# Attention with a second, filling stream of matmuls: maxima earlier, stores later, more filler

## Chip, cores, metric

One core of one Trainium2 chip runs the kernel. The metric is the device time of one execution in microseconds (us); lower is better. Engines: PE multiplies matrices, DVE, ACT and POOL work on elements, and SP does nothing here but issue DMAs from one queue, in order.

## The reference, cut to what matters

```python
u = rms_norm(x, norm_g)                      # [2048, 1024]
q, k, v, z_att, f, z_ssd, xbc, dt, x_lru, z_lru = split(u @ w_in)
# A) 8 heads of 64, causal, with a forget bias c = cumsum(log_sigmoid(f + forget_b))
logits = q_i @ k.T * 64**-0.5 + (c_i[:, None] - c[None, :])   # masked above the diagonal
y_att = softmax(logits) @ v * silu(z_att)                     # 512 columns
y_ssd = ...                                                    # 1024 columns, gated norm at the end
y_lru = ...                                                    #  512 columns
out = x + concat([y_att, y_ssd, y_lru]) @ w_out                # w_out [2048, 1024]
```

## The kernel before

Everything is float32; a product is made of three float32r matmuls, of high and low halves (h·h, h·l, l·h). Up to about 1250 us of the span the kernel makes the projections, the LRU and SSD branches and the normalised q and k, and leaves them in DRAM. This part is not touched. Then follow two streams of work that share the PE.

**Attention.** A *unit* `j` is a head `h` and a block `sb` of 256 queries; there are 64, the blocks of head 0 and head 7 in falling order and those of the six heads between in rising order. A unit has `sb + 1` *tasks* `(j, kp)`, one for each 256 keys: 288 in all. `score(j, kp)` makes the transposed scores of a task in a PSUM bank `T` (L987, L988), ACT takes their exponential twice (L996 rounded into `ph`, L997 in full), and DVE takes the difference `pl` (L998). Three tasks later (`AVL`) `av` multiplies with the values into `O` (L1040, L1042), and `finish` closes the unit: the sums of the exponentials go in through `ah` and `al` (L1050, L1051), the result `to` (L1054 to L1058) and the sums `su` go to DRAM (L1061, L1063). The diagonal task of a unit, its last, uses 384 of the bank's 512 columns and gets a mask matmul (L992).

The exponential needs each query's extreme score beforehand. `maxima(j)` makes plain scores `S` on PE (L945) in chunks of 512 keys, and DVE reduces each (L955, or L950 for the chunk at the diagonal, L953 over the chunks) into a column of `mz`. `flip(j)` transposes `mz` on PE (L969) into a PSUM tile `pm`, and two ACT casts (L970, L971) put it as a row into `q`, which the first score matmul of unit `j` reads (L987). `S` and `pm` share two PSUM banks (`psS`), `T` has three, `O` two, the filler one.

**Filler.** `sweeps()` is a generator that makes the output projection: per 128 tokens `t` and half `n` of the columns, four *rounds* of three matmuls of 512 columns (L1112 to L1114, `po`), and DVE adds the result to `xr`, which came from DRAM and goes back there (`pt_d`; L1133, L1118 or L1120, L1135). `mix` loads and splits the left operand (`mt`, `mh`, `ml`). Sweep 0 takes the LRU rows, sweep 1 half of the SSD rows; then the other half and the attention rows alternate. There are 512 rounds. `fill` draws rounds while attention runs, `FIRST + tasks * RATE // 288` of them, and the rest follow when attention is over. `load_wo` loads a fourth of `w_out` in eight pieces and splits each on ACT and DVE.

The order of the instructions on each engine is set by the framework's scheduler, from the order in which the code creates them; each engine then runs its list in order. What a list holds is shown below where it matters.

Of the kernel before, what the change touches and what calls it, by code (L numbers as in the profile page):

```python
# [18 lines left out]
P = 128  # L19
# [11 lines left out]
FIRST = 12  # L31
RATE = 260
LEAD = 3
# [5 lines left out]
AVL = 3  # L39
LT = 2  # L40
NDV = 3
# [7 lines left out]
def hybrid_block(ctx, tc, x, norm_g, w_in, q_norm_g, k_norm_g, forget_b, ssd_conv_w, ssd_conv_b,  # L49
# [338 lines left out]
    def group_za(pool, vpool, g):  # L388
        w = weights([(C_ZA + g * 256, 256)])
        for tb in range(4):  # L390
            for mm in range(2):
                m = g * 2 + mm
                ps = proj_ch(w, mm, tb, f"pza{m}_{tb}")
                if g == 1 and tb == 2 and mm == 0:
                    anchor[1] = anchor[0]
                th = pool.tile([P, 512], F32, name=f"th{m}_{tb}", tag="sqq")
                A.activation(th, ps, AF.Tanh, scale=0.5)
                zt = vpool.tile([P, 512], F32, name=f"zt{m}_{tb}", tag="qk")
                V.scalar_tensor_tensor(zt, th, 1.0, ps, op0=ALU.add, op1=ALU.mult)
                dma(za_d[m][:, tb * 512:(tb + 1) * 512], zt)  # L400

# [374 lines left out]

    for i in range(2):
        G.memset(mzs[i], 0.0)
    for i in range(2):
# [41 lines left out]

    def load_wo(k0, half, lastp, tag):
        ws = {}
        pl = [(k0 + i, n) for i in range(4) for n in range(2)]
        tags = [f"u{p}{half}_{k}" for k in range(KD) for p in "hl"]
        for j, (k, n) in enumerate(pl):
            h = upa.tile([P, 512], F32R, name=f"woh{k}_{n}", tag=tags[2 * j])
            l = upa.tile([P, 512], F32R, name=f"wol{k}_{n}", tag=tags[2 * j + 1])
            cs = slice(n * 512, n * 512 + 512)
            row = w_out[k * P:(k + 1) * P, cs]  # L830
            if j + 1 < len(pl):
                raw = [upa.tile([P, 512], F32, name=f"wor{k}_{n}", tag=tags[2 * j + 3])]
            else:
                raw = [lastp.tile([P, 256], F32, name=f"wor{k}_{n}_{i}", tag=tag) for i in range(2)]
            m = 512 // len(raw)
            for i, r in enumerate(raw):
                dma(r, row[:, i * m:(i + 1) * m])
                hc, lc = h[:, i * m:(i + 1) * m], l[:, i * m:(i + 1) * m]
                if 4 <= k < 12:
                    g = c1("sg", k - 4)  # L840
                    A.activation(hc, r, AF.Copy, scale=g)
                    V.scalar_tensor_tensor(lc, r, g, hc.bitcast(F32), op0=ALU.mult,
                                           op1=ALU.subtract)
# [4 lines left out]
        return ws  # L848

    with tpool(name="ap", bufs=2) as pool, tpool(name="ap1", bufs=1) as ap1, \  # L850
            tpool(name="qkp", bufs=QB) as qkp:
        for p in range(4):
# [41 lines left out]
            if p == 2:  # L894
                load_head(0)
                load_q(0)
    ws = [load_wo(12, 0, wrp, "wr"), load_wo(8, 1, wrp, "wr")]
    pb.close()

    pcx = ExitStack()  # L900
    o2 = cx.enter_context(tpool(name="o2", bufs=2))
    o3 = cx.enter_context(tpool(name="o3", bufs=LEAD))
    a1 = cx.enter_context(tpool(name="a1", bufs=1))
# [9 lines left out]
    make_k2(1)  # L913
    make_q(a1)
    U = [{} for _ in units]

    def maxima(j):
# [6 lines left out]
        def first():  # L924
            if j % 2 and j + 1 < len(units):
                load_q(j + 1)
            za = a3.tile([64, 256], F32, name=f"za{j}", tag="za")
            u["za"] = za
            p, b = divmod(h, 2)
            dma(za, za_d[p][b * 64:b * 64 + 64, sb * 256:(sb + 1) * 256])  # L930
            if j % 8 == 2 and h < 7:
                load_head(h + 1)

        def chunk(i, c0):
# [5 lines left out]
            o = (sb % 2) * 256 + i * P  # L940
            col = mzs[j % 2][:, 64 + 32 * i:65 + 32 * i]
            if c0 == 0 and nc_ > 1:
# [5 lines left out]
            if c0 + w == n:  # L948
                jk = a1.tile([P, 512], F32, name=f"jk{j}_{i}", tag="jk")
                V.tensor_tensor_reduce(jk[:, 0:w], ps[:, 0:w], zm[:, 640 - w:640], 1.0, 3.0e38,  # L950
                                       ALU.add, ALU.min, to)
                if nc_ > 1:
                    V.tensor_reduce(col, u["mc"][:, 0:nc_], axis=AX.X, op=ALU.min)  # L953
            else:
                V.tensor_reduce(to, ps, axis=AX.X, op=ALU.min)  # L955
# [6 lines left out]

    def flip(j):

        h, sb = units[j]
        q3 = qs_[j // 2][0]
        o = (sb % 2) * 256
        pm = psS.tile([P, P], F32, name=f"pm{j}", tag="S")
        T.transpose(pm[0:97, :], mzs[j % 2][:, 0:97], ident)  # L969
        A.copy(q3[96:97, o:o + P], pm[64:65, :])  # L970
        A.copy(q3[96:97, o + P:o + 256], pm[96:97, :])  # L971

    def score(j, kp):
# [71 lines left out]
    def finish(j):  # L1045
# [17 lines left out]
        dma(s_d[qt, h:h + 1, :].rearrange("i o t -> o i t"),  # L1063
            su.rearrange("o (i t) -> o i t", i=2))
        if h == 7:

            sr = a2.tile([16, P], F32, name=f"sr{j}", tag="sr")
# [10 lines left out]
    def mix(t, k0, kind):  # L1078
# [5 lines left out]
        if kind == "att":  # L1084
            dma(mt, at_d[:, :, tsl].rearrange("i p t -> p i t"))
            rb = o2.tile([P, 4, P], F32, name=f"rb{t}", tag="xr")
            for b in range(2):
# [34 lines left out]
    SEQ = ((12, "lru"), (8, 1), (4, 0), (0, "att"))  # L1122

    def sweeps():
        for i in range(2):
            cur = mix(0, *SEQ[i])
            for t in range(NT):
                nxt = mix(t + 1, *SEQ[i]) if t + 1 < NT else None
                tsl = slice(t * P, (t + 1) * P)
                for n in range(2):  # L1130
                    cs = slice(n * 512, n * 512 + 512)
                    xr = o2.tile([P, 512], F32, name=f"xr{t}_{n}_{i}", tag="xr")
                    dma(xr, (pt_d if i else xf)[tsl, cs])  # L1133
                    yield from half(t, n, i, cur, xr)
                    dma(pt_d[tsl, cs], xr)  # L1135
                cur = nxt
            ws.append(load_wo(SEQ[i + 2][0], i, o2, "mt"))

        xs = {}
        work = [(t, 2) for t in range(LEAD)]  # L1140
# [6 lines left out]
        for w, (t, i) in enumerate(work):  # L1147
            tsl = slice(t * P, (t + 1) * P)
            if i == 2:
                xs[t] = o3.tile([P, D], F32, name=f"xo{t}", tag="xo")  # L1150
                dma(xs[t], pt_d[tsl, :])
            if i == 3 and cur is None:
                cur = mix(t, *SEQ[3])
            nxt = None
            for n in range(2):
                cs = slice(n * 512, n * 512 + 512)
                if n == 1 and w + 1 < len(work) and (work[w + 1][1] == 2 or "X" in pso):
                    nxt = mix(work[w + 1][0], *SEQ[work[w + 1][1]])
                yield from half(t, n, i, cur, xs[t][:, cs])
                if i == 3:  # L1160
                    dma(of[tsl, cs], xs[t][:, cs])
            cur = nxt

    filler = sweeps()
    with tc.high_priority(offset=HP), tc.issue_after(anchor[1].ins):
        steps = maxima(0)
        for j, st in enumerate(steps):
            st()
            for _ in range(FIRST * (j + 1) // len(steps) - FIRST * j // len(steps)):
                next(filler)  # L1170
        flip(0)
    count = [0, FIRST]
    recent = []

    def fill(ins):
        count[0] += 1
        recent.append(ins)
        want = FIRST + count[0] * RATE // 288
        while want > count[1]:
            count[1] += 1  # L1180
            with tc.issue_after(recent[max(0, len(recent) - 1 - LAG)].ins):
                next(filler)

# [8 lines left out]
    flips = {begin[j] - 1: j for j in range(1, len(units))}  # L1192
    for i in range(len(tasks) + AVL + 1):
        ins = None
        if i < len(tasks):
            ins = score(*tasks[i])
            if i in flips:
                flip(flips[i])
            for f in at.get(i, ()):
# [7 lines left out]
        if ins is not None:  # L1207
            fill(ins)
    pcx.close()
    pso["P"] = cx.enter_context(tpool(name="psP2", bufs=6, space=PSUM))  # L1210
# [33 lines left out]
```

## Time and profile before

| | us |
|---|---|
| median of 3 runs (lowest, highest) | 2072.73 (2069.95, 2073.84) |
| profiled execution, its time | 2065.23 |
| profiled execution, span | 2063.5 |
| PE busy, share of the span | 1970.9, 96% |
| DVE, ACT, POOL busy | 1303.0, 1007.7, 803.1 |
| first maxima of the first unit (L945) start | 1231.3 |
| last mask matmul (L992) starts | 1889.7 |

A row of the groups reads: line, engine, operation, output<-inputs, shapes, count | busy us, mean ns of one | idle us of the engine just before them, and what ended it. A row of the waits reads: who waited <- for whom: us in total, times, longest. A row of the windows gives a stretch, its length, busy us and instructions of each engine, the clock that PE was granted (1.00 is full speed), and the share and rate of the DMA engines. A matmul's end in the profile is modelled, and one that streams starts long before the one ahead of it has ended.

### The profile page before, as it was taken

To read this page: it belongs to the slowest core of one execution; us is meant where nothing else is said; L and a number is where in the kernel's file an instruction comes from. 1 tells how busy PE (TensorE), PEld (TensorE's weight loads), DVE (VectorE), ACT (ScalarE), POOL (GpSimd) and SP (SyncE) were. 2 spreads that over 40 slices of the span, in tenths; PEclk is the share of its full clock that TensorE was granted. 3 is DMA by queue.
4 is the path that set the end of the run, shared out by engine and by line. 5 is a ranking of instruction groups with operands and counts; after the bars stand their busy time and mean duration, and the time that the engine had idled before them with its cause. 6 is when DMAs were issued, how large, how long until landed. Compare 5 with 4: busy or idle time off the path is not lost.

```text
span 2063.5 us, 35018 instructions
## 1 busy us (share of the span) xinstructions
PE 1970.9 (96%) x11941; PEld 1713.8 (83%) x11941; DVE 1303.0 (63%) x2576; ACT 1007.7 (49%) x2177; POOL 803.1 (39%) x918
## 2 busy tenths in 40 slices
PE   7999999999999999898999998989899999898999
PEld 6898888898989898787887986878777888777887
DVE  6748555555464736777667264777777777787343
ACT  7524444544443534544444242666576666675110
POOL 0100000233231415555553003768677777776110
PEclk9999999999999999999999998999999999999999
DMA  5322223121312145667756465355365455342554
GB/s 186 97 82 70 70 79 95 41 74 34 99 31 75 31 133 175 190 176 222 207 163 177 109 194 165 115 152 149 108 187 142 126 151 152 105 141 82 173 170 136
DMA packets 260466, 261.32 MB, mean 127 GB/s; under 512 B 26772, under 2 KB 198832, under 8 KB 258736
## 3 DMA queue, kind: packets, MB, share of 16 engines
q1 hardware_dynamic: 260128, 259.05, 42.7%
q8 instruction: 95, 1.56, 0.3%
q0 software_dynamic: 160, 0.03, 0.1%
q14 instruction: 83, 0.68, 0.1%
HBM read 164.22 MB, written 94.77 MB: 126 GB/s over the span
## 4 chain that ended last, share of the span: by engine, by line
PE 41%; DMA 6%; DVE 4%; ACT 4%; issue 2%; POOL 2%; SPq 0%; DVEq 0%; POOLq 0%; ACTq 0%
PE po L1112 5%; PE po L1113 5%; PE po L1114 5%; PE T L987 3%; PE T L988 3%; PE S L945 2%; PE O L1040 2%; PE O L1042 2%; PE py L691 2%; PE pza L358 1%; PE pza L359 1%; PE pza L357 1%; DMA ab<-acs_d 1%; PE pqk L341 1%; PE pqk L343 1%
## 5 line engine op out<-in xcount | busy, mean ns | idle before, releaser
L998 DVE TENSOR_TENSOR pl<-T,ph 128x512 fp32r<-128x512 f32 (+1 forms) x288 | 187.3, 655 | 48.8 <-ACT T L997 46.3
L1112 PE MATMUL po<-woh,mh 128*128 128x512 f32 x512 | 204.1, 399 | 7.5 <-DVE xr L1120 4.6
L996 ACT ACTIVATE ph<-T 128x512 fp32r<-128x512 f32 (+1 forms) x288 | 165.1, 573 | 88.7 <-PE T L988 60.5
L1113 PE MATMUL po<-wol,mh 128*128 128x512 f32 x512 | 202.7, 396 | 0.0
L1114 PE MATMUL po<-woh,ml 128*128 128x512 f32 x512 | 202.6, 396 | 0.0
L1010 POOL TENSOR_TENSOR ac<-ac,ph 128x512 f32<-128x512 f32 x120 | 156.1, 1301 | 23.1 <-ACT ph L996 17.2
L997 ACT ACTIVATE T<-T 128x512 f32<-128x512 f32 (+1 forms) x288 | 164.9, 572 | 0.0
L987 PE MATMUL T<-q,k 128*128 128x256 f32 x576 | 150.0, 287 | 9.6 <-ACT q L971 6.8
L955 DVE TENSOR_REDUCE mc<-S 128x1 f32<-128x512 f32 x192 | 130.2, 685 | 41.8 <-PE S L945 41.3
L357 PE MATMUL pxx<-uh,wh 128*128 128x512 f32 x384 | 152.8, 400 | 1.7 <-ACT uh L302 1.7
L358 PE MATMUL pxx<-ul,wh 128*128 128x512 f32 x384 | 153.1, 399 | 0.0
L345 PE MATMUL pqk<-wh,ul 128*128 128x256 f32 x512 | 151.0, 295 | 0.0
L359 PE MATMUL pxx<-uh,wl 128*128 128x512 f32 x384 | 150.9, 395 | 0.0
L1040 PE MATMUL O<-ph,vv 128*128 128x256 f32 x576 | 149.0, 280 | 0.9 <-ACT ph L996 0.4
L343 PE MATMUL pqk<-wl,uh 128*128 128x256 f32 x512 | 148.8, 291 | 0.0
L341 PE MATMUL pqk<-wh,uh 128*128 128x256 f32 x512 | 148.6, 291 | 0.0
L1042 PE MATMUL O<-pl,vv 128*65 128x256 f32 x576 | 142.2, 279 | 3.4 <-DVE pl L998 2.8
L413 DVE SCALAR_TENSOR_TENSOR accx<-rtx,cv,accx 128x512 f32<-128x512 f32 x144 | 108.0, 752 | 57.3 <-ACT accx L410 54.5
L343 PE MATMUL pzs<-wl,uh 128*128 128x256 f32 x512 | 143.8, 281 | 0.0
L988 PE MATMUL T<-qx,kx 128*128 128x256 f32 x576 | 143.7, 283 | 0.0
L345 PE MATMUL pzs<-wh,ul 128*128 128x256 f32 x512 | 143.4, 280 | 0.0
L341 PE MATMUL pzs<-wh,uh 128*128 128x256 f32 x512 | 143.0, 281 | 0.0
(353 smaller groups left out, 5711.8 us busy)
## 6 DMA issues: line engine op xcount, KB each, us to landing
ab<-acs_d SPq DMA_DIRECT2D x64, 256.0 KB
pt_d<-xr SPq DMA_DIRECT2D x64, 256.0 KB
wr<-in_w_in_dram SPq DMA_DIRECT2D x112, 128.0 KB
xt<-in_x_dram SPq DMA_DIRECT2D x16, 512.0 KB
xs_d<-stx SPq DMA_DIRECT2D x32, 256.0 KB
v_d<-vs SPq DMA_DIRECT2D x32, 256.0 KB
wr<-in_w_in_dram SPq DMA_DIRECT2D x128, 64.0 KB
zs_d<-zs SPq DMA_DIRECT2D x32, 256.0 KB
```

The costliest lines, as they stand in the source:

```text
L341: T.matmul(ps[:, i, :], h[k][:, sl], wh[k], start=(k == 0 and i == 0), stop=False, skip_group_check=True)
L343: T.matmul(ps[:, i, :], h[k][:, sl], wl[k], start=False, stop=False, skip_group_check=True)
L345: ins = T.matmul(ps[:, i, :], l[k][:, sl], wh[k], start=False, stop=last, skip_group_check=True)
L358: T.matmul(ps, wh[k][:, ms], ul[tb][k], start=False, stop=False)
L987: T.matmul(ps, k2[:, ks], q3[:, qs], start=(jj == 0), stop=False, skip_group_check=True)
L988: ins = T.matmul(ps, kx[:, ks], qx[:, qs], start=False, stop=True, skip_group_check=True)
L998: V.tensor_tensor(pl[:, 0:n], pt[:, 0:n], ph[:, 0:n].bitcast(F32), op=ALU.subtract)
L1040: T.matmul(po[:, qs], vv[:, kt, 0:128], ph[:, cs], start=(kt == 0), stop=(kt == 2 * sb + 1), skip_group_check=True)
L1042: T.matmul(po[0:65, q2], vv[:, kt, 64:129], pl[:, cs], start=False, stop=False, skip_group_check=True)
L1112: T.matmul(ps, mh[:, j, :], h, start=(j == 0), stop=False)
L1113: T.matmul(ps, mh[:, j, :], l, start=False, stop=False)
L1114: T.matmul(ps, ml[:, j, :], h, start=False, stop=(j == 3))
```

## The change

- `LT` 2 to 3: a unit's maxima are made one task earlier. Four `mz` tiles of 97 columns instead of two of 128; `za` gets a fourth buffer.
- `flip(j + 1)` writes its transpose into columns 384 to 512 of the bank of the diagonal scores of unit `j`, right behind the mask matmul, instead of into a bank of `psS`.
- `load_head` of the next head moves from unit 2 of a head to unit 4.
- `finish` and the filler hand their stores to `later`, which issues them 1 or 2 tasks on; the reciprocals' round trip through DRAM follows the sums' store, and `ready` tells the filler 4 tasks later that the attention rows of this block can be mixed, which it now may do ahead.
- `xr` is loaded one half ahead, into four buffers instead of two.
- `load_wo` becomes a generator that loads a piece ahead and splits one piece at a time: the second fourth of `w_out` during sweep 0, no longer before attention; the third during sweep 1, the last behind it.
- `RATE` 260 to 290, and `MORE = 2` further rounds for each of the last `END = 14` tasks.
- The discarded output `jk` of L950 is bfloat16, and the store of `za` in `group_za` is created one step later.

```diff
-RATE = 260
+RATE = 290
-LT = 2
+LT = 3
+END = 14
+MORE = 2
...
-    mzs = [kc.tile([P, P], F32, name=f"mz{i}") for i in range(2)]
+    mzs = [a1.tile([P, 97], F32, name=f"mz{i}") for i in range(4)]
...
-            if j % 8 == 2 and h < 7:
+            if j % 8 == 4 and h < 7:
                 load_head(h + 1)
...
-    def flip(j):
+    def flip(j, pm):
...
-        pm = psS.tile([P, P], F32, name=f"pm{j}", tag="S")
-        T.transpose(pm[0:97, :], mzs[j % 2][:, 0:97], ident)
+        T.transpose(pm[0:97, :], mzs[j % 4], ident)
         A.copy(q3[96:97, o:o + P], pm[64:65, :])
         A.copy(q3[96:97, o + P:o + 256], pm[96:97, :])
...
             ins = T.matmul(pv, idr, zmt.unsqueeze(1).broadcast_to([P, 2, P]), start=False,
                            stop=True, skip_group_check=True)
+            if j + 1 < len(units):
+                flip(j + 1, pt[:, 384:512])
...
-        dma(at_d[p][b * 64:b * 64 + 64, cs], to)
...
+        def store():
+            dma(at_d[p][b * 64:b * 64 + 64, cs], to)
+            dma(s_d[qt, h:h + 1, :].rearrange("i o t -> o i t"),
+                su.rearrange("o (i t) -> o i t", i=2))
...
+            later(lambda: ready.add(sb), 4)
+
+        later(store, 1)
...
+    def later(f, n=2):
+        if clock[0] is None:
+            f()
+        else:
+            late.append((clock[0] + n, f))
...
-                    xr = o2.tile([P, 512], F32, name=f"xr{t}_{n}_{i}", tag="xr")
-                    dma(xr, (pt_d if i else xf)[tsl, cs])
+                    load_xr(t * 2 + n + 1)
+                    xr = xrs.pop(t * 2 + n)
                     yield from half(t, n, i, cur, xr)
-                    dma(pt_d[tsl, cs], xr)
+                    def store(xr=xr, t=t, n=n):
+                        dma(pt_d[t * P:(t + 1) * P, n * 512:n * 512 + 512], xr)
...
+                        later(store)
...
+                    if t > 0 and n == 0:
+                        next(more, None)
...
-                if n == 1 and w + 1 < len(work) and (work[w + 1][1] == 2 or "X" in pso):
-                    nxt = mix(work[w + 1][0], *SEQ[work[w + 1][1]])
+                if n == 1 and w + 1 < len(work):
+                    t1, i1 = work[w + 1]
+                    if i1 == 2 or t1 // 2 in ready:
+                        nxt = mix(t1, *SEQ[i1])
...
-        want = FIRST + count[0] * RATE // 288
+        want = FIRST + count[0] * RATE // 288 + MORE * max(0, count[0] - 288 + END)
```

Three places in the engines' lists show what this moves.

PE, around the transpose for unit 36 (a middle unit of head 4), before. `O35` is the output of unit 35, `T36_0` the first scores of unit 36, `S37` the maxima of unit 37:

```order
L945 MATMUL S37_0_0_18382<-k20_9585,q30_9577 128x512
L1042 MATMUL O35_18418<-pl35_3_18399,vv4_16897 65x256
L1040 MATMUL O35_18418<-ph35_3_18398,vv4_16897 128x128
L1042 MATMUL O35_18418<-pl35_3_18399,vv4_16897 65x128
L969 MATMUL pm36_18411<-ident_102,mz0_9573 97x128
L945 MATMUL S37_0_512_18415<-k20_9585,q30_9577 128x512
L987 MATMUL T36_0_18437<-q30_9577,k20_9585 128x256
L988 MATMUL T36_0_18437<-qx0_9580,kx4_16896 128x256
```

and after, from the mask matmul of unit 35 on:

```order
L1011 MATMUL T35_3_18417<-zmt_9571,idr_9569 128x2x128
L988 MATMUL T35_3_18417<-ident_102,mz0_13447 97x128
L1063 MATMUL O35_18448<-pl35_0_18328,vv4_17078 65x256
L1061 MATMUL O35_18448<-ph35_0_18327,vv4_17078 128x256
L1063 MATMUL O35_18448<-pl35_0_18328,vv4_17078 65x256
L1061 MATMUL O35_18448<-ph35_1_18361,vv4_17078 128x256
L1139 MATMUL po5_0_8_18521<-woh8_0_13806,mh5_8_18235 128x512
L1140 MATMUL po5_0_8_18521<-wol8_0_13807,mh5_8_18235 128x512
L1071 MATMUL O34_18337<-ah34_18304,onr_9566 65x256
L1141 MATMUL po5_0_8_18521<-woh8_0_13806,ml5_8_18236 128x512
L1139 MATMUL po5_0_8_18521<-woh9_0_14288,mh5_8_18235 128x512
```

Before, one matmul stands between the transpose and the scores that need it; after, `T36_0` is the eighteenth row behind the transpose.

ACT at the same place, before (`q30` is the casts' target):

```order
L996 ACTIVATE ph35_3_18398<-T35_3_18392 128x384
L997 ACTIVATE T35_3_18392<-T35_3_18392 128x384
L970 CAST q30_9577<-pm36_18411 1x128
L971 CAST q30_9577<-pm36_18411 1x128
L1021 CAST ah35_18407<-w35_18403 128x256
```

and after:

```order
L989 CAST q30_9573<-T35_3_18417 1x128
L990 CAST q30_9573<-T35_3_18417 1x128
L1017 ACTIVATE ph35_3_18426<-T35_3_18417 128x384
L1018 ACTIVATE T35_3_18417<-T35_3_18417 128x384
L1017 ACTIVATE ph36_0_18472<-T36_0_18467 128x512
```

The casts have moved ahead of the exponentials of the diagonal task, whose bank they read.

SP in sweep 0, before (`to15`, `su17` are results and sums of units 15 and 17):

```order
L930 DMA za19_15868<-za_d1_78 64x256
L1061 DMA at_d_97<-to16_15979 64x256
L1135 DMA pt_d_13500<-xr10_0_0_16003 128x512
L1133 DMA xr10_1_0_16134<-in_x_dram 128x512
L1096 DMA mt13_12_16557<-lr_d3_101 128x128
L1063 DMA s_d_93<-su17_16069 2x1x128
L1133 DMA xr11_0_0_16298<-in_x_dram 128x512
```

and after:

```order
L1190 DMA pt_d_13455<-xr9_0_0_15423 128x512
L1086 DMA s_d_93<-su13_15520 2x1x128
L1179 DMA xr11_0_0_15885<-in_x_dram 128x512
L1085 DMA at_d_97<-to13_15519 64x256
L950 DMA za17_15761<-za_d1_78 64x256
L1190 DMA pt_d_13455<-xr9_1_0_15540 128x512
L1179 DMA xr11_1_0_16040<-in_x_dram 128x512
```

Before, the store of half 10_0 stands ahead of the load of half 10_1, which the filler needs next; after, the loads stand four halves ahead of the stores (11_0 beside 9_0).

In PE's whole list the last matmul of attention, `O63<-al63`, is row 10335 before and row 10443 after: 108 filler matmuls, 36 rounds, have moved from behind attention to ahead of its end.

More of the change, by code (lines that the diff above doesn't have):

```diff
@@ L819, in load_q, with load_wo, load @@
         qs_[j // 2] = q3, qx
-    def load_wo(k0, half, lastp, tag):
-        ws = {}
+    def load_wo(ws, k0, half, last):
         pl = [(k0 + i, n) for i in range(4) for n in range(2)]
         tags = [f"u{p}{half}_{k}" for k in range(KD) for p in "hl"]
+        raw = {}
+        def load(j):
+            k, n = pl[j]
+            if j + 1 < len(pl):
+                raw[j] = [upa.tile([P, 512], F32, name=f"wor{k}_{n}", tag=tags[2 * j + 3])]
+            else:
+                raw[j] = last(f"wor{k}_{n}")
+            m = 512 // len(raw[j])
+            for i, r in enumerate(raw[j]):
+                dma(r, w_out[k * P:(k + 1) * P, n * 512 + i * m:n * 512 + (i + 1) * m])
+        load(0)
+        yield
         for j, (k, n) in enumerate(pl):
+            if j + 1 < len(pl):
+                load(j + 1)
             h = upa.tile([P, 512], F32R, name=f"woh{k}_{n}", tag=tags[2 * j])
             l = upa.tile([P, 512], F32R, name=f"wol{k}_{n}", tag=tags[2 * j + 1])
[L829 to L837, printed above, removed]
+            m = 512 // len(raw[j])
+            for i, r in enumerate(raw[j]):
                 hc, lc = h[:, i * m:(i + 1) * m], l[:, i * m:(i + 1) * m]
@@ L847, in load_wo @@
             ws[k, n] = (h, l)
-        return ws
+            yield
     with tpool(name="ap", bufs=2) as pool, tpool(name="ap1", bufs=1) as ap1, \
@@ L896, in hybrid_block @@
                 load_q(0)
-    ws = [load_wo(12, 0, wrp, "wr"), load_wo(8, 1, wrp, "wr")]
+    ws = [{}, {}, {}, {}]
+    for _ in load_wo(ws[0], 12, 0, lambda nm: [
+            wrp.tile([P, 256], F32, name=f"{nm}_{i}", tag="wr") for i in range(2)]):
+        pass
     pb.close()
@@ L914, in hybrid_block @@
     make_q(a1)
+    mzs = [a1.tile([P, 97], F32, name=f"mz{i}") for i in range(4)]
+    for mz in mzs:
+        G.memset(mz, 0.0)
     U = [{} for _ in units]
@@ L1122, in hybrid_block, with run_late, wo_last, load_xr @@
     SEQ = ((12, "lru"), (8, 1), (4, 0), (0, "att"))
+    late = []
+    clock = [0]
+    ready = set()
+    def later(f, n=2):
+        if clock[0] is None:
+            f()
+        else:
+            late.append((clock[0] + n, f))
+    def run_late(t):
+        clock[0] = t
+        while late and (t is None or late[0][0] <= t):
+            late.pop(0)[1]()
+    def wo_last(nm):
+        return [o4.tile([P, 512], F32, name=nm, tag="xr")]
     def sweeps():
         for i in range(2):
+            more = load_wo(ws[i + 1], SEQ[i + 1][0], 1 - i, wo_last)
+            xrs = {}
+            def load_xr(j):
+                t, n = divmod(j, 2)
+                if t < NT:
+                    xrs[j] = o4.tile([P, 512], F32, name=f"xr{t}_{n}_{i}", tag="xr")
+                    dma(xrs[j], (pt_d if i else xf)[t * P:(t + 1) * P, n * 512:n * 512 + 512])
+            load_xr(0)
             cur = mix(0, *SEQ[i])
@@ L1128, in sweeps @@
                 nxt = mix(t + 1, *SEQ[i]) if t + 1 < NT else None
-                tsl = slice(t * P, (t + 1) * P)
                 for n in range(2):
-                    cs = slice(n * 512, n * 512 + 512)
-                    xr = o2.tile([P, 512], F32, name=f"xr{t}_{n}_{i}", tag="xr")
-                    dma(xr, (pt_d if i else xf)[tsl, cs])
+                    load_xr(t * 2 + n + 1)
+                    xr = xrs.pop(t * 2 + n)
                     yield from half(t, n, i, cur, xr)
-                    dma(pt_d[tsl, cs], xr)
+                    def store(xr=xr, t=t, n=n):
+                        dma(pt_d[t * P:(t + 1) * P, n * 512:n * 512 + 512], xr)
+                    if t < NT - 1:
+                        later(store)
+                    else:
+                        store()
+                    if t > 0 and n == 0:
+                        next(more, None)
                 cur = nxt
-            ws.append(load_wo(SEQ[i + 2][0], i, o2, "mt"))
+            for _ in more:
+                pass
+        more = load_wo(ws[3], SEQ[3][0], 1, wo_last)
         xs = {}
@@ L1152, in sweeps @@
             if i == 3 and cur is None:
+                while t // 2 not in ready:
+                    yield True
                 cur = mix(t, *SEQ[3])
@@ L1156, in sweeps @@
                 cs = slice(n * 512, n * 512 + 512)
-                if n == 1 and w + 1 < len(work) and (work[w + 1][1] == 2 or "X" in pso):
-                    nxt = mix(work[w + 1][0], *SEQ[work[w + 1][1]])
+                if n == 1 and w + 1 < len(work):
+                    t1, i1 = work[w + 1]
+                    if i1 == 2 or t1 // 2 in ready:
+                        nxt = mix(t1, *SEQ[i1])
                 yield from half(t, n, i, cur, xs[t][:, cs])
+                for _ in range(2):
+                    next(more, None)
                 if i == 3:
-                    dma(of[tsl, cs], xs[t][:, cs])
+                    later(lambda t=t, cs=cs: dma(of[t * P:(t + 1) * P, cs], xs[t][:, cs]))
             cur = nxt
@@ L1177, in fill @@
         recent.append(ins)
-        want = FIRST + count[0] * RATE // 288
+        want = FIRST + count[0] * RATE // 288 + MORE * max(0, count[0] - 288 + END)
         while want > count[1]:
+            with tc.issue_after(recent[max(0, len(recent) - 1 - LAG)].ins):
+                if next(filler):
+                    break
             count[1] += 1
-            with tc.issue_after(recent[max(0, len(recent) - 1 - LAG)].ins):
-                next(filler)
     tasks = [(j, kp) for j, (h, sb) in enumerate(units) for kp in range(sb + 1)]
@@ L1191, in hybrid_block @@
             at.setdefault(a + i * (b - a) // len(st), []).append(f)
-    flips = {begin[j] - 1: j for j in range(1, len(units))}
     for i in range(len(tasks) + AVL + 1):
         ins = None
+        run_late(i)
         if i < len(tasks):
             ins = score(*tasks[i])
-            if i in flips:
-                flip(flips[i])
             for f in at.get(i, ()):
```

27 lines of the change are left out of this document (15 added, 12 removed).

## Prediction

> **What bounds the kernel now.** I read first the page's head and the 40 slices, then the windows of the attention stage and of what follows it, then who waited for whom on PE, last the timeline at single waits.
>
> ```profile
> PE 1970.9 (96%) x11941; PEld 1713.8 (83%) x11941; DVE 1303.0 (63%) x2576; ACT 1007.7 (49%) x2177; POOL 803.1 (39%) x918
> ...
> 1250.00:1894.40 644.40, 590.61 (x3693) 512.02 (x3694) 479.28 (x1119) 415.59 (x948) 470.88 (x523) 0.97 0.50 139
> 1900.00:2060.00 160.00, 159.32 (x703) 131.57 (x702) 66.53 (x150) 17.44 (x28) 16.80 (x13) 1.00 0.50 157
> ```
>
> PE bounds the whole. Behind attention (1900 to 2060) it streams: 703 matmuls of 512 columns in 160.00 us, 0.2276 us each, 0.4445 ns a column. In attention (1250 to 1894.4) it doesn't. The work there, counted from the code: scores, their low part, both `O` products and the maxima have 139,264 columns each (8 heads x 136 pairs of 128-blocks x 128), `ah` and `al` 32,768, masks 16,384, transposes 8,192, and 272 filler rounds 417,792: together 1,171,456 columns, at 0.4445 ns 520.7 us. The stage takes 644.4, so 123.7 us aren't work. PE's idle time holds 53.8 of them (644.40 less 590.61). No other engine is full (DVE 479 of 644).
>
> ```profile
> PE pm L969 <- DVE mz L953: 14.1, 17, 3.9
> PE T L987 <- ACT q L971: 6.8, 18, 1.8
> PE S L945 <- DVE mc L955: 5.6, 9, 1.6
> PE po L1112 <- DVE xr L1120: 4.6, 1, 4.6
> PE S L945 <- DMA q<-qh_d: 3.7, 3, 2.9
> PE S L945 <- ACT q L971: 3.6, 10, 0.7
> PE O L1042 <- DVE pl L998: 2.8, 4, 1.0
> PE O L1050 <- ACT ah L1021: 2.1, 3, 0.9
> PE po L1112 <- DVE xr L1118: 1.9, 3, 1.5
> ...
> PE O L1051 <- POOL al L1022: 1.6, 2, 1.1
> PE S L945 <- DVE mz L950: 1.6, 4, 0.4
> ```
>
> A second part is the clock: seven spells in the stage run at half of it.
>
> ```profile
> 1253.00:1260.30 7.30, 6.55 (x15) 4.58 (x15) 1.68 (x6) 1.43 (x3) 5.28 (x5) 0.53 0.61 198
> 1281.00:1288.00 7.00, 4.92 (x14) 3.87 (x14) 2.01 (x7) 0.00 (x0) 0.73 (x1) 0.54 0.45 146
> 1359.00:1366.20 7.20, 6.14 (x25) 5.08 (x26) 3.25 (x10) 2.28 (x8) 2.10 (x3) 0.53 0.43 140
> 1451.00:1455.00 4.00, 4.00 (x17) 3.76 (x18) 2.42 (x6) 3.25 (x7) 1.87 (x2) 0.57 0.64 182
> 1550.00:1554.00 4.00, 3.74 (x15) 3.14 (x16) 4.00 (x7) 2.59 (x7) 3.07 (x5) 0.57 0.22 55
> 1560.00:1564.20 4.20, 4.01 (x18) 3.73 (x19) 4.11 (x9) 2.67 (x6) 3.22 (x4) 0.59 0.32 89
> 1683.00:1687.00 4.00, 3.93 (x18) 3.67 (x19) 1.74 (x5) 1.13 (x4) 3.16 (x5) 0.57 0.48 148
> ```
>
> Length times what the clock lacks: 3.4 + 3.2 + 3.4 + 1.7 + 1.7 + 1.7 + 1.7 = 16.9 us (rounded up where idle overlaps). The rest, 123.7 - 53.8 - 16.9 = 53 us, is in matmuls that don't stream though the profile calls PE busy.
>
> ```profile
> L987 PE MATMUL T<-q,k 128*128 128x256 f32 x576 | 150.0, 287 | 9.6 <-ACT q L971 6.8 <-DVE pl L998 1.8 <-DMA mt<-lr_d 0.4
> ```
>
> Such a matmul is drawn with 287 ns, but a streamed one of 256 columns takes 114, so pauses up to some 0.17 us don't show as idle.
>
> **The change, part by part.** PE's total work stays. The 36 rounds that move into attention (36 x 3 x 0.2276 = 24.6 us) are worth nothing by themselves: they lengthen one stage and shorten the other. Only the 123.7 us can shrink, and each term below is a part of them.
>
> A. Maxima earlier, transpose ahead of the scores by other work: the waits of `pm` on `mz` (14.1) and of `T` and `S` on the casts (6.8, 3.6), 24.5 us.
>
> ```profile
> 1437.94 0.30 PE L969 MATMUL pm<-ident,mz 128*97 128x128 f32 x1
> 1437.99 0.48 PE L945 MATMUL S<-k,q 96*128 96x512 f32 x1
> 1438.85 0.33 PE L945 MATMUL S<-k,q 96*128 96x128 f32 x1 [0.38 <-ACT q L971]
> ...
> 1438.27 0.26 ACT L970 CAST q<-pm 1x128 fp32r<-1x128 f32 x1 [0.89 <-PE pm L969]
> 1438.54 0.26 ACT L971 CAST q<-pm 1x128 fp32r<-1x128 f32 x1
> ```
>
> From the transpose to the use of the row are 0.9 us. In PE's list fewer than 0.9 us of streamed columns stand between them at 43 of 63 boundaries before and at 13 after; the last maxima stand on average 3.2 us of columns ahead of the transpose before and 7.0 after. By the counts 10.4 us of cast waits fall to about 3 and 14.1 to 2: 19 saved, between 10 (the waits halve) and 24.5.
>
> B. The transposes leave the two banks of `S`. The waits of `S` on reductions (5.6 and 1.6) go, except 1.9 in the stage's first ten us: 5 saved, between 0 and 7.2. In PE's list a bank of the pair is wanted again within 1 us of columns 65 times before, 5 times after.
>
> C. Sums loaded ahead, stores late, head load later: `po` on `xr` (4.6, 1.9) and `S` on the load of `q` (3.7), 10.2 us.
>
> ```profile
> 1443.47 0.33 SPq L1135 DMA_DIRECT2D pt_d<-xr  x1
> 1443.85 0.42 SPq L1133 DMA_DIRECT2D xr<-in_x_dram  x1
> ...
> 1447.87 0.75 DVE L1120 TENSOR_TENSOR xr<-xr,po 128x256 f32<-128x256 f32 x2 [2.31 <-DMA xr<-in_x_dram]
> ```
>
> The load of the old sums is queued behind a store that waits for DVE, lands about 4 us later, and DVE stands still with `pl` and maxima queued behind. The load no longer follows that store: 8 saved, between 3 and 10.2. Past `at_d`, `s_d` and `pt_d` stores each load only gets earlier; what is later is the store, which nobody reads for many tasks, save the last block's sums, whose trip 204 rounds of filler (512 less 272 and 36) cover.
>
> D. The other waits (`O` on `pl`, `ah`, `al`): 6.5 us. They sit mostly in the last short units, which get extra filler: 2 saved, between 0 and 6.5.
>
> E. Clock. The spell at 1253 belongs to the start, which stays; of the other 13.5 us two thirds go with the waits ahead of them: 9, between 0 and 13.5.
> The Trainium skill ("TensorE: Matmul & The Clock Gate", section "Why this matters for your kernels") asks for no PE gap above about 3 us. By that rule only the two waits of 3.9 and 4.6 us above would start spells, and this term would be about 5 and the sum 40. The trace disagrees: it has seven spells, and in the one at 1451 PE is busy 4.00 of 4.00 us; so I keep 9.
>
> F. The 53 us of unseen pauses. Part is fixed (a fraction of a tenth of a us at changes of operand), and filler in between helps the rest: 5, between 0 and 25.
>
> G. New costs. The second fourth of `w_out` is now split during attention.
>
> ```profile
> L842 DVE SCALAR_TENSOR_TENSOR wol<-wor,cv,woh 128x512 fp32r<-128x512 f32 (+1 forms) x18 | 14.7, 826 | 8.6 <-ACT woh L841 8.3
> L841 ACT ACTIVATE woh<-wor,cv 128x512 fp32r<-128x512 f32 (+1 forms) x18 | 11.5, 672 | 9.0 <-DMA wor<-in_w_out_dram 7.4 <-PE po L1114 1.6
> ```
>
> Half of these, 7 us on DVE and 6 on ACT, move from ahead of attention, where PE streams anyway, into it, a piece at a time, and 36 rounds bring 9 `xr` updates of 0.75 us (the row of 1447.87). DVE goes from 479 to about 493 of some 625. I charge 4, between 0 and 13. The bfloat16 `jk` and the `za` store count nothing: L950 reads PSUM as before, and SP's list has the `za` stores in the same order. The fourth `za` buffer and the narrower `mz` change no instruction on PE's path.
>
> Sum: 19 + 5 + 8 + 2 + 9 + 5 - 4 = 44 us. The profiled execution took 2065.23 (span 2063.5) and would take 2021; it lies 7.5 us under the median of the runs, 2072.73, which becomes **2029**.
>
> **The rivals.** 1. *Transpose holds the exponential* (slower). The diagonal `ph` now stands behind casts that wait for the transpose, and it for `mz`.
>
> ```profile
> ACT q L970 <- PE pm L969: 67.1, 34, 9.1
> ```
>
> ACT stood 67.1 us at these casts before; what is new is that an exponential of the same bank is behind them. At 24 boundaries 0.5 to 7.6 us of columns, 57 in all, lie between mask and transpose. If every one became PE idle, the 44 would turn into 13 lost: 2086. It takes 44 of the 57 to break even. Against it: the next use of `pl` is three tasks on, and 39 boundaries have no delay.
> The Trainium skill ("PSUM — Partial Sum Buffer", section "PSUM bank collisions raise a hardware error") says that two engines may not touch one bank and quadrant at once, so software must put the transpose and the exponential one after the other; no run here shows the overlap, and the trace decides only what the order costs.
> 2. *Only the transfers' part counts*: waits at the boundaries return in other places, as DVE and ACT lists are as full as before; C, half of E and little else: 8 + 5 = 13, so 2060.
> 3. *Filler fills nearly everything*: A to E at their upper ends (24.5 + 7.2 + 10.2 + 6.5 + 13.5) and 13 of F: 75, so 1998.
> 4. *The change doesn't do what it says*: filler stalls on its single bank, since `xr` takes 0.75 us of DVE per half and 9 more halves lie in attention; if 0.5 us of it show at each of 77 halves, 39 are lost, so no change, 2068. Against it: that wait is 6.5 us over 68 halves before.
>
> **How the numbers follow.** Chances: forecast 0.56 (own range 2012 to 2046, where A, E and F lie at half or one and a half of my values), rival 2 0.17, rival 3 0.13, rival 1 0.07, rival 4 0.07. The range of 8 in 10 takes in most of rivals 2 and 3: 2004 to 2060. About 0.2% (4 us) can be told from no change. Slower: 0.06 (rival 1 beyond its point); same: 0.07; faster: 0.87.
>
> **What would show it.** Right: `pm` on `mz` and `T` on the casts under 6 us together; no `po` on `xr` above 2 us; two to four spells of half clock; PE idle between first scores and last `O` near 25 us; the last mask matmul near 1870, with 204 rounds behind it. Wrong: ACT waiting for the transpose well above 67 us with PE waiting for `T` banks or `pl`; `po` waiting for `xr` in every half; DVE above nine tenths busy. The forecast fails most likely in E and F, which have no row of their own for what ends them.

## The result, and the profile after

Median 2023.6 us over 4 runs (2019.02 to 2024.83) against 2071.87 (2069.95 to 2073.84) for the kernel before: ratio 0.9763, 95% interval 0.9744 to 0.9782, so 49 us faster. A repetition, in another comparison, gave 0.9767 (0.9746 to 0.9788). The forecast was 2029 (2004 to 2060). The profiled execution took 2024.83, its span 2023.1, 40.4 less than the span before.

PE's line of the page, after:

```profile
PE 1953.6 (97%) x11941; PEld 1708.9 (84%) x11941; DVE 1302.0 (64%) x2573; ACT 1005.7 (50%) x2174; POOL 803.6 (40%) x920
```

The windows of the attention stage and of what follows it, after:

```profile
1258.30:1868.70 610.40, 591.85 (x3800) 526.82 (x3800) 484.68 (x1138) 417.54 (x952) 473.18 (x525) 0.99 0.54 153
1868.70:2023.10 154.40, 142.00 (x612) 115.53 (x612) 59.77 (x135) 15.54 (x26) 14.91 (x12) 0.99 0.45 142
```

The stage takes 610.40 us where it took 644.40, though it holds 36 more rounds. PE idles 18.6 us of it (610.40 less 591.85; before 53.8), and the clock is 0.99 (before 0.97). Behind attention the gain turns round, as the same stretch of before shows:

```profile
1894.40:2063.50 169.10, 164.92 (x721) 136.05 (x720) 69.42 (x155) 18.07 (x30) 17.52 (x14) 0.99 0.49 152
```

There PE idled 4.2 us, the program's end included; after, it idles 12.4.

The waits of PE from 1240 to 1900, after, longest sums first:

```profile
PE po L1139 <- DVE xo L1145: 7.6, 5, 3.3
PE S L965 <- DVE mc L975: 5.3, 5, 2.5
PE O L1061 <- DVE to L1078: 2.9, 1, 2.9
PE T L1006 <- DVE pl L1019: 2.6, 2, 2.4
PE T L1006 <- ACT q L990: 2.1, 5, 0.6
PE po L1139 <- DVE xr L1147: 1.2, 2, 0.8
...
PE po L1139 <- DVE xr L1145: 0.6, 1, 0.6
PE O L1061 <- ACT ph L1017: 0.5, 1, 0.5
```

The transpose waits for `mz` nowhere (14.1 before), the scores wait 2.1 us for the casts (6.8), and the load of `q` has gone from the first rows (3.7). At the head stands a wait that before did not have: `po` for `xo`, the output of the last sweep, 6.2 of its 7.6 us behind attention.

And ACT's wait at the casts, the one that rival 1 rested on:

```profile
ACT q L989 <- PE T L988: 71.1, 41, 4.9
```

It is as long as before (67.1), with an exponential queued behind it, and PE has no row that answers to it above 2.6 us.

### The profile page after: what moved, and what is told of

It reads as the page before. It is cut to its first block, busy times and chain, and to the rows that moved or that the text cites. A ratio compares the mean times of both kernels' runs of the same rounds, so it can differ in the third digit from the quotient of the medians.

```text
span 2023.1 us, 34947 instructions
## 1 busy us (share of the span) xinstructions
PE 1953.6 (97%) x11941; PEld 1708.9 (84%) x11941; DVE 1302.0 (64%) x2573; ACT 1005.7 (50%) x2174; POOL 803.6 (40%) x920
## 4 chain that ended last, share of the span: by engine, by line
PE 42%; DMA 6%; DVE 3%; ACT 2%; issue 2%; POOL 1%; SPq 0%; DVEq 0%; POOLq 0%; ACTq 0%
PE po L1139 5%; PE po L1140 5%; PE po L1141 5%; PE T L1006 3%; PE T L1007 3%; PE O L1061 3%; PE S L965 3%; PE O L1063 2%; DMA ab<-acs_d 2%; PE pza L360 1%; PE pza L361 1%; PE pza L359 1%; PE py L698 1%; PE pqk L347 1%; PE pqk L343 1%
## 5 line engine op out<-in xcount | busy, mean ns | idle before, releaser
L1061 PE MATMUL O<-ph,vv 128*128 128x256 f32 (+1 forms) x576 | 149.5, 279 | 3.5 <-DVE to L1078 2.9
```

The source lines that it names most:

```text
L1061: T.matmul(po[:, qs], vv[:, kt, 0:128], ph[:, cs], start=(kt == 0), stop=(kt == 2 * sb + 1), skip_group_check=True)
```

## Where the time went, run by run

The prediction's account of the stage can be made for each run. *Rest* is the time from the last projection matmul to the last `O`, less the columns at 0.4445 ns, counted as in the prediction (520.7 us, and 0.683 for each round beyond 272); *idle* is PE's, *half* the time at half clock (half of it is lost), and *hidden* what is left of the rest: pauses under some 0.17 us inside what counts as busy. One profiled execution each; the others of a kernel differ from it by up to some 10 us (the profiled ones of x1, 2052.28, and x15, 2051.98, are the slowest of their five). (The bounds differ a little from the windows above, so before has 124.6 here for the prediction's 123.7.)

| kernel | median us | ratio (95%) | stage | rest | idle | half | hidden | rest behind attention |
|---|---|---|---|---|---|---|---|---|
| before | 2071.87 | 1 | 645.3 | 124.6 | 54.5 | 34.1 | 53.0 | 1.0 |
| after | 2023.6 | 0.9763 (0.9744, 0.9782) | 611.1 | 65.8 | 19.2 | 17.1 | 38.1 | 11.0 |
| x1_maxima | 2045.69 | 0.9876 (0.9853, 0.99) | 626.8 | 106.1 | 45.0 | 47.8 | 37.2 | -0.6 |
| x2_transfers | 2053.47 | 0.9919 (0.9897, 0.9941) | 630.6 | 109.9 | 43.8 | 28.5 | 51.9 | 2.0 |
| x3_filler | 2072.48 | 1.001 (0.9993, 1.0027) | 674.0 | 131.4 | 57.7 | 54.9 | 46.3 | 0.9 |
| x4_less_filler | 2016.45 | 0.9732 (0.9705, 0.9758) | 593.4 | 72.7 | 24.4 | 11.8 | 42.4 | 0.3 |
| x5_old_bank | 2041.69 | 0.9872 (0.9855, 0.9889) | 619.1 | 98.4 | 39.2 | 24.6 | 46.9 | 0.7 |
| x13_two_bufs | 2040.24 | 0.9862 (0.9842, 0.9882) | 622.0 | 101.3 | 41.7 | 37.5 | 40.8 | 1.0 |
| x15_two_edits | 2042.35 | 0.9881 (0.9861, 0.9902) | 625.8 | 105.1 | 41.9 | 44.4 | 41.0 | -0.1 |
| x16_three_edits | 2027.23 | 0.98 (0.9774, 0.9826) | 601.4 | 80.7 | 26.8 | 23.9 | 42.0 | 0.0 |
| x12_spread | 2012.12 | 0.9733 (0.9715, 0.9752) | 588.9 | 68.2 | 20.4 | 16.0 | 39.8 | 2.6 |
| x11_more0 | 2012.02 | 0.9723 (0.9705, 0.9741) | 611.5 | 68.9 | 23.0 | 17.1 | 37.4 | 1.1 |
| x18_spread_290 | 2005.45 | 0.9693 (0.9673, 0.9713) | 602.5 | 59.9 | 16.6 | 6.8 | 39.9 | -0.1 |

Before against after: the rest of the stage shrinks by 58.8 us, behind attention 10.0 are lost, and the untouched stages ahead ended 8.3 us later in this execution (1256.8 against 1248.5; the other runs lie between 1248 and 1258): 58.8 - 10.0 - 8.3 = 40.5, the difference of the spans to 0.1.

## The experiments

In the expectations, M is the theory of the prediction: the gain is the waits at the unit boundaries and transfers, by parts, and filler is worth little. F is its rival: the added filler fills the holes. T, another, puts the whole gain down to the loads that stand behind stores. B came up after the first four runs: the transpose's bank and the buffers of `xr` carry nearly all, each only together with the other.

**Each part alone.** x1: the kernel before with the earlier maxima, the transpose in the bank of the diagonal scores and the head load at unit 4 (four `mz` tiles, a fourth `za` buffer and the bfloat16 `jk` go with it). x2: the changed kernel with the transpose in a bank of `S`, `LT` 2, two `mz` tiles and the old amount of filler, so with little but the transfers' part.

```diff
 x1, against before                         x2, against after
-LT = 2                                    -RATE = 290, MORE = 2, LT = 3
+LT = 3                                    +RATE = 260, MORE = 0, LT = 2
+            flip(j + 1, pt[:, 384:512])   -            flip(j + 1, pt[:, 384:512])
-                flip(flips[i])            +                flip(flips[i], psS.tile(...))
```

> The kernel before with the maxima part alone: LT 3, four mz tiles, the transpose in the bank of the diagonal scores, the head load two units later (it moves with LT, since the maxima of unit 2 now begin before the last scores of the head before). Before is 2072, after 2024. Theory M (the waits at the unit boundaries and the clock spells behind them are most of the gain, terms A, B and half of E): 28 us less than before, 2044; pm on mz and T on the casts together under 6 us. Rival F (extra filler fills whatever idle there is): 2067. Rival T (loads behind stores on the DMA queue are the cause): 2067.

> The kernel after without the maxima part and without more filler (LT 2, two mz tiles, transpose in a bank of S, RATE 260, MORE 0): what is left over before are late stores, sums loaded ahead, w_out as a generator, the later head load and the attention rows mixed ahead. Theory M: 10 us less than before, 2062, with pm on mz still near 14 us and po on xr under 3 us. Rival F: 2072, no change. Rival T: 30 us less, 2042.

x1 came out at 0.9876, 26 us; x2 at 0.9919, 17 us. Added they give 42, and the two together without more filler (x4, below) gave 55, though the later head load is in both: the parts need each other. M's forecast of 2044 for x1 holds; for x2 it had 2062, 9 us too slow. PE's first waits in x1 and in x2:

```profile
PE po L1113 <- DVE xr L1119: 11.9, 3, 5.1
PE po L1113 <- DVE xr L1121: 11.8, 3, 5.8
```

```profile
PE pm L988 <- DVE mz L973: 9.3, 14, 1.5
PE T L1006 <- ACT q L990: 7.5, 17, 2.3
```

In x1 the boundary waits are gone and the wait for the old sums is 23.7 us where before had 6.5; in x2 that wait is gone and the boundary waits stay. PE no longer stops at the boundary, so it comes to the filler's bank sooner, and the load of `xr` is not there yet.

**One ingredient taken out.** x5 and x13 start from x4, the changed kernel with the old amount of filler. x5 puts the transpose back into a bank of `S`, and with it the transpose and its two casts back to where the code of before makes them, behind the exponentials of the diagonal task; all else stays. x13 gives `xr` two buffers instead of four, with all the new code of the loads and stores in place.

```diff
 x5                                         x13
-            flip(j + 1, pt[:, 384:512])   -o4 = ...tc.tile_pool(name="o4", bufs=4)
+                flip(flips[i], psS.tile()) +o4 = ...tc.tile_pool(name="o4", bufs=2)
```

> x4_less_filler (the kernel after with the filler of before, 2016) with the transpose back in a bank of S; LT 3 and four mz tiles stay. Theory B (of the maxima part only the bank counts, since PE's list hardly moves with LT or the tiles): 30 us or more over x4, about 2050, the waits on the casts back above 8 us. Rival L (the maxima's lead of one task and the four mz tiles count): within 8 us of x4, 2024 at most.

> x4_less_filler with two xr buffers instead of four; late stores and the load one half ahead in the code stay. Theory B (of the transfers part the buffers count: with four of them the list has the loads far ahead of the stores, with two each load stands behind the store of the half before): 25 us over x4, about 2042, with po waiting for xr above 10 us. Rival S (late stores and early loads in the code count): within 5 us of x4, 2021 at most.

x5: 0.9872, x13: 0.9862, against 0.9732 with both: the bank, with the place of the transpose, is worth 29 us (0.0140 of 2070), the buffers 27. x13 came as B had it; x5 is 8 us faster than B's 2050 and 18 slower than L's 2024. In x5 the boundary waits do not return as they were; this is PE's list there, and then the row of the maxima in before, in x5, in x4 and in after:

```profile
PE O L1069 <- ACT ah L1040: 8.3, 5, 5.2
PE S L965 <- ACT q L990: 6.8, 12, 0.9
PE S L965 <- DVE mc L975: 5.4, 12, 1.6
```

```profile
L945 PE MATMUL S<-k,q 96*128 96x512 f32 (+2 forms) x320 | 120.6, 390 | 14.8 <-DVE mc L955 5.6 <-DMA q<-qh_d 3.7 <-ACT q L971 3.6
```

```profile
L965 PE MATMUL S<-k,q 96*128 96x512 f32 (+2 forms) x320 | 117.9, 389 | 14.1 <-ACT q L990 6.8 <-DVE mc L975 5.4 <-DVE mz L970 0.7
```

```profile
L965 PE MATMUL S<-k,q 96*128 96x512 f32 (+2 forms) x320 | 111.1, 373 | 3.9 <-DVE mc L975 2.5 <-DVE mz L970 0.8
```

```profile
L965 PE MATMUL S<-k,q 96*128 96x512 f32 (+2 forms) x320 | 109.2, 375 | 6.0 <-DVE mc L975 5.3 <-DMA q<-qh_d 0.2
```

With the transpose in its banks the maxima idle PE 14 us ahead of them and are drawn 390 ns long; without it 4 to 6 us and 373 to 375 ns. The busy time of the same 320 matmuls falls by 11.4 us from before to after (spells of half clock lengthen them too). The table's last but one column points the same way: with the old bank (before, x2, x3, x5) 46 to 53 us are hidden, with the new one 37 to 42 in all nine others. The one pair that differs in this edit alone is x5 and x4: 46.9 against 42.4 us hidden, and 117.9 against 111.1 us of busy maxima. So some 4 to 7 us of unseen pauses go with the edit. The greater part of its cost can be seen: of the 25.7 us by which the stage of x5 is longer, 14.8 are idle time of PE and 6.4 are clock. That these are waits of `S` and `pm` for each other's banks is not shown apart: in x4 the casts (1453.60, for one) run ahead of the diagonal exponentials (1454.16), in x5 behind them (1461.25 behind 1457.30), and no run moves the bank without the place.

x13 shows the other half. A wait of `po` early in the stage, by the timeline of SP, DVE and PE:

```profile
1273.17 0.60 SPq L1179 DMA_DIRECT2D xr<-in_x_dram  x1
...
1278.19 0.81 DVE L1147 TENSOR_TENSOR xr<-xr,po 128x256 f32<-128x256 f32 x2 [3.94 <-DMA xr<-in_x_dram]
...
1279.15 0.47 PE L1139 MATMUL po<-woh,mh 128*128 128x512 f32 x1 [3.87 <-DVE xr L1147]
```

The load is issued at 1273.17, 5.0 us before DVE can add; DVE stands 3.94 us with the maxima behind it, and PE 3.87. The code still writes the load one half ahead, but with two buffers it can only be issued once the store of the half before last has freed one: from 1266 to 1282 SP stands twice, 9.0 us in all, with such a load until `pt_d<-xr` has landed. The buffers make the load early, not the place of the line.

**Few ingredients put in.** x15 gives the kernel before the new bank (and with it the new place of the transpose) and four buffers for `xr` alone; x16 adds the move of the head load from unit 2 to unit 4.

```diff
 x15, against before
+    o4 = cx.enter_context(tpool(name="o4", bufs=4))
-                    xr = o2.tile(...)
+                    xr = o4.tile(...)
+                flip(j + 1, pt[:, 384:512])
 x16, against x15
-            if j % 8 == 2 and h < 7:
+            if j % 8 == 4 and h < 7:
```

> The kernel before with two edits alone: the transpose in the bank of the diagonal scores, and four buffers for xr and rb (jk in bfloat16 and one buffer less for sr make the room). No late stores, LT 2, two mz tiles, RATE 260. Theory B: like x4_less_filler within 6 us, 2016 to 2022. Rivals L and S: the missing parts bring at least half of the 54 us, so 2040 or more.

> The kernel before with three edits: the transpose in the diagonal scores' bank, four buffers for the loaded sums, and the head load at unit 4; LT 2, the stores' and loads' code and RATE 260 stay. Theory (the third ingredient that the two edits lacked is the place of the head load): the wait of S on the load of q (16.1 us with two edits) falls under 3 us and the time to 2016 to 2024, like the changed kernel with less filler. Rival (the missing part lies in LT 3, the late stores or the loads written ahead): S on the load of q may go, but the time stays at 2035 or above, with other waits in its place.

x15 reached 0.9881, 25 us, and B fell: two edits are not enough. PE's first wait in x15, and in x16:

```profile
PE S L946 <- DMA q<-qh_d: 16.1, 6, 3.6
```

```profile
PE T L987 <- DVE pl L1000: 5.2, 8, 1.3
```

In x15 the maxima wait for the next block of `q`, 3.7 us in all before; with the head load two units later this wait is not among PE's first, and x16 stands at 0.98, 41 us. That is the third ingredient, though 2027.23 misses the range forecast for it, 2016 to 2024, by 3 us. The remaining 14 us to x4 (0.9800 against 0.9732; the intervals do not meet) lie in what x4 has beyond x16: `LT` 3, the four `mz` tiles, the stores' order, the loads written ahead, the pieces of `w_out` by a generator and the attention rows mixed ahead. Of these, `LT` and `mz` together differ between x5 and x2 (0.9872 and 0.9919, about 10 us with the old bank); what each is worth with the new bank was not run apart.

**The filler.** x3: the kernel before with `RATE` 290. x4: the changed kernel with `RATE` 260 and `MORE` 0. x11: the changed kernel with `MORE` 0 alone. x17 is the changed kernel again, beside x11.

```diff
 x3, against before      x4, against after      x11, against after
-RATE = 260             -RATE = 290            -MORE = 2
+RATE = 290             +RATE = 260            +MORE = 0
                        -MORE = 2
                        +MORE = 0
```

> The kernel before with RATE 290 alone: 32 more filler rounds inside attention by the list of PE. Theory M: PE's work is the same and the waits are mostly in order, so 5 us less, 2067. Rival F: most of the 22 us of moved rounds fall into idle time, 2050 or less. Rival T: 2072.

> The kernel after with RATE 260 and MORE 0: maxima and transfers as after, the filler as before. Theory M: 8 us more than after, 2032. Rival F: 25 us more, 2049. Rival T: 2024, as after.

> The changed kernel with RATE 290 but without the MORE rounds of the last 14 tasks. Theory (MORE is what costs: its rounds run on the filler's single bank where little else is left on PE, 7.6 us of po on xo right behind attention): those waits fall to about 3 us and the time to 2014 to 2018. Rival (RATE 290 costs as much by itself, or the difference of 7 us to RATE 260 is only from execution to execution): 2021 to 2026, as the changed kernel.

> The changed kernel itself, unaltered, in the same comparison as the other three, so that a few us can be told apart. If the extra filler costs what one run said, its ratio stands at 0.976 to 0.977 and the kernels without MORE at 0.972 to 0.974; if that difference was chance, all are within 0.002 of each other.

x3 gained nothing (1.0010, 0.9993 to 1.0027), and F is out; M had 5 us of gain there, also a miss. x4 was a miss for M and F: less filler is not slower, and at 2016.45 rather faster, though its interval and that of after overlap. x11 says why: 2012.02 (2009.89 to 2013.45), 2 us below the range of its theory, where the changed kernel had 2020.11 (2017.87 to 2025.49) beside it. `RATE` 290 or 260 makes no difference (0.9723 and 0.9732), `MORE` costs 8 us; x17 stands where it was forecast. PE behind attention, from the timeline of after (the matmuls that began with a wait):

```profile
1871.98 0.63 PE L1139 MATMUL po<-woh,mh 128*128 128x512 f32 x1 [3.33 <-DVE xo L1145]
1877.63 0.47 PE L1139 MATMUL po<-woh,mh 128*128 128x512 f32 x1 [1.06 <-DVE xo L1145]
1881.57 0.47 PE L1139 MATMUL po<-woh,mh 128*128 128x512 f32 x1 [0.94 <-DVE xo L1147]
1885.07 0.50 PE L1139 MATMUL po<-woh,mh 128*128 128x512 f32 x1 [0.53 <-ACT mh L1118]
1892.66 0.47 PE L1139 MATMUL po<-woh,mh 128*128 128x512 f32 x1 [1.86 <-DVE xo L1145]
1896.19 0.50 PE L1139 MATMUL po<-woh,mh 128*128 128x512 f32 x1 [0.53 <-ACT mh L1126]
```

and the window behind attention in x11:

```profile
1863.60:2011.30 147.70, 143.36 (x625) 118.23 (x625) 61.10 (x135) 15.56 (x26) 15.55 (x13) 0.99 0.47 150
```

`MORE` draws up to 28 rounds more from `sweeps()` while the tasks are being made, and a half drawn then gets the filler's single bank; what is drawn after them gets six (`psP2`). In PE's list only 4 of those rounds stand ahead of the last `O` (308 rounds there, 304 without `MORE`). The other 24, six halves, run behind attention with nothing beside them, each waiting until DVE or ACT has dealt with the half before: six waits, 8.3 us. In x11 PE has no wait above 0.7 us there.

**The pieces of `w_out`.** In the changed kernel's list the pieces of the third and last fourths do not come one at a time: their loads and splits stand together where the buffers of the fourth before come free. Seven of the eight splits of the third run from 1510 to 1525 us, all eight of the last from 1760 to 1780. The kernel before has such bursts too (splits from 1540 to 1558 and from 1844 to 1858). x12 (from x4) and x18 (from x11) tie each split to the filler's latest result by a product with zero.

```diff
 x12 from x4, x18 from x11
-                if 4 <= k < 12:
-                    g = c1("sg", k - 4)
+                if 4 <= k < 12 or tie[0] is not None:
+                    g = c1("sg", k - 4) if k >= 4 else ones[:, 0:1]
+                    if tie[0] is not None:
+                        V.scalar_tensor_tensor(gt, tie[0], 0.0, g, op0=ALU.mult, op1=ALU.add)
...
+                    tie[0] = xr[:, 0:1] if i else None
```

> x4_less_filler with the third and the last fourth of w_out split piece by piece: each piece's scale is a column that DVE makes from the filler's last result (16 instructions of 128x1 more), so that ACT and DVE can't take eight pieces at once. In x4 the units around 1510 to 1545 and 1654 to 1674 hold 16.6 us of lost time where quiet units of that length lose 5. Theory: that and the clock spell behind it, 10 us less than x4, 2006. Rival (the bursts lie beside other waits, and the new column only adds a wait on DVE): 2016 or more.

> The changed kernel without MORE, and with each split of a piece of the third and last fourths of w_out tied to the filler's latest result, so that they can't come in a burst. Theory (with RATE 290 the bursts at 1500 and 1770 cost some 4 to 8 us of single waits): 2008 to 2014, the fastest of all. Rival (as with RATE 260, what the bursts cost comes back in other waits): the same as the kernel without MORE, within 4 us.

With the old amount of filler nothing came of it (0.9733 and 0.9732), where the theory had 10 us: the single waits of the two bursts went, others came, one of 3.8 us on the casts among them. With `RATE` 290 it is 2005.45 (2002.06 to 2009.28), ratio 0.9693 (0.9673 to 0.9713), 6.6 us under x11 in the same comparison; the runs' ranges do not meet, the intervals just do. It is the fastest kernel of this study, 2.5 us below the range of its theory. The two stretches in x11 and in x18:

```profile
1500.00:1530.00 30.00, 24.82 (x147) 21.59 (x146) 22.43 (x47) 20.46 (x44) 19.98 (x22) 0.89 0.64 199
1765.00:1795.00 30.00, 26.10 (x168) 22.75 (x167) 27.41 (x52) 17.24 (x37) 21.92 (x22) 1.00 0.14 45
```

```profile
1500.00:1530.00 30.00, 30.00 (x204) 27.20 (x204) 25.17 (x58) 23.93 (x55) 26.45 (x30) 1.00 0.85 244
1765.00:1795.00 30.00, 28.77 (x188) 25.43 (x187) 27.68 (x59) 20.90 (x46) 22.30 (x22) 1.00 0.22 74
```

In the first, PE is idle 5.2 us less, and the clock is whole instead of 0.89, which is worth another 3.3. Why the same tie gives nothing with 32 rounds fewer is open.

## Why the prediction was right or wrong, point by point

- **That only the non-work of the stage counts: right.** 32 more rounds alone are worth nothing (x3; x11 against x4).
- **A, 19 of 24.5 us at the boundaries.** In after 2.1 us are left of the three rows, 22 gone. But a wait taken away was not a gain by itself: in x1, with the same edit, 17 us more appeared on `xr`. The sum was right only because C was in the same change.
- **B, 5 us for the two banks: far too small.** Of the visible waits hardly anything went (`S` on the reductions 7.2, after 5.3). Taking the bank and the place of the transpose back out costs 29 us: 14.8 us of idle time of PE, 6.4 of clock and 4.4 hidden in the stage of x5 against x4. Little of the idle time stands at the rows that B priced: `S` on the reductions is 5.4 in x5 and 2.5 in x4, while `O` on `ah` (8.3 against 3.3), `S` on the casts (6.8 against none) and `pm` on the reductions (5.5 against none) came up. The failed step is the pricing of a bank by its own rows in the waits.
- **C, 8 of 10.2 us.** The waits for `xr` fell from 6.5 to 1.8 and the one for `q` from the list. The price was about right for the kernel as it was (x2, with the old bank and lead, idles 10.7 us less than before) and wrong for the kernel as it became: x13 puts it at 27 us, x1 shows 23.7 on `xr`, x15 16.1 on `q`. These were second in line behind the boundaries. The prediction named the head load's move with them, on a 3.7 us row, and x16 against x15 makes it 17 us (0.0081 of 2070).
- **D, 2 of 6.5 us.** `O` on `to` and `ph` came in the place of `O` on `pl` and `ah`: 3.4 in their first rows, so nearer 3 than 2.
- **E, 9 us of clock: right in size.** Half clock went from 34.1 to 17.1 us, 8.5 gained, with four spells in the stage where "two to four" stood. The reason was read wrongly at one point: the spell at 1451, shown as one with PE busy throughout, began right behind a wait of 3.9 us, which the window began too late to hold. The rule of the Trainium skill ("TensorE: Matmul & The Clock Gate", "Why this matters for your kernels") was right on that spell. On others it is not: three of after's follow or fall into waits of 2.43, 2.49 and 2.92 us, and of the 74 spells counted in the last section 32 have no wait of 2 us or more at their start or in the 1.5 us ahead of it.
- **F, 5 us of unseen pauses: measured 14.9.** It was priced low because no row stood for it. By x5 against x4 some 4 to 7 of it go with the bank and the place of the transpose; for the rest no run names a cause.
- **G, 4 us of new costs: 10, and at another place.** The forecast had the second fourth of `w_out` move into attention; in the list 7 of its 8 pieces stay ahead. The third and last fourths come in bursts, but they did so before. What is new is that `MORE`'s rounds stall behind attention. That "behind attention PE streams" was taken over from the profile of before and no longer held.
- **The end of the stage** was forecast near 1870 with 204 rounds behind it. The last mask matmul starts at 1863.8, with 612 matmuls, 204 rounds, in the window behind.
- **Rivals.** 1 (the transpose holds the exponential) did not come: ACT waits 71.1 us there, as before, and PE's waits on `pl` and `ph` are 3.1. 2 (transfers alone, 2060) is too slow by 36 us. 3 (1998) was beyond this change, but x18 at 2005.45 shows it was not beyond this kernel. 4 came true at another place: the single bank stalls, not in attention but behind it, and for 8 us, not 39.

Term by term: A to D were 34 us together, and PE's idle time in the stage fell by 35.3; E was 9 against 8.5. A gain, F, was 10 us too small and a cost, G, 6 too small. These two errors partly cancel, and the stages ahead vary by some us (8.3 between the two profiled executions), so that the total came within 6 us of the forecast is in part luck. A to D came right as a sum, not one by one: B and C were priced on rows that grew when a part was put in or taken out alone.

## What to carry to other kernels

A row of waits gives what is late first, not what the repair is worth: behind it stands the next, so price a group of edits by asking what PE meets when the first wait is gone, and test them by taking one out as well as by putting one in. Two kinds of tile in one small pool can cost more than the waits at those tiles show; take one out, and compare the idle time of the whole engine and the busy time of the same matmuls. And look at the list, not the code, for where a piece, a load or a round lands: the buffers decided it here, and work drawn early keeps the small pool it was drawn with.

## What the runs showed of the hardware

How long a wait of PE brings a spell of half clock: over 14 profiled executions of these kernels, from 1262 to 2000 us, I counted PE's gaps and those in or within 1.5 us behind which a spell begins.

| gap of PE, us | gaps | with a spell |
|---|---|---|
| 0.5 to 1 | 126 | 11 |
| 1 to 1.5 | 44 | 10 |
| 1.5 to 2 | 21 | 8 |
| 2 to 2.5 | 15 | 11 |
| 2.5 to 3.5 | 19 | 16 |
| over 3.5 | 16 | 15 |

So there is no sharp bound here; from 2 us on a wait mostly brings a spell, 42 times in 50. Of the 74 spells 47 last 3.4 us, 24 last 6.8 and 3 last 10.2, so one costs 1.7, 3.4 or 5.1 beside the wait. Two of after, by its windows:

```profile
1776.60:1780.00 3.40, 3.40 (x16) 3.11 (x15) 3.40 (x8) 1.19 (x3) 1.29 (x1) 0.50 0.00 0
1872.10:1875.50 3.40, 3.40 (x9) 2.62 (x10) 1.28 (x3) 0.00 (x0) 0.72 (x1) 0.51 0.03 8
```

PE is busy throughout both, at a clock of 0.50; the waits of 2.43 and 3.33 us stand just ahead of them. That is why windows for a spell should begin some us before it.
